# A long convolution by small Fourier transforms: whole fp32 operands in place of high and low parts, and all two-operand work on VectorE

## The chip, the cores and the metric

The kernel runs on one core of a Trainium2 chip. The metric is the device time of one execution in microseconds (us). Five engines work side by side, each through its own queue in order: TensorE (PE in the profile, with its weight loads under PEld), VectorE (DVE), ScalarE (ACT), GpSimd (POOL) and SyncE (SP), which here only issues DMA transfers. Engines wait for each other through semaphores.

## The reference, cut to what matters

The program is a chain of network layers: attention, a recurrent layer, then a second block. In the recurrent layer one branch is a "Hyena" operator: two long convolutions over 1024 positions for each of 512 channels, each followed by a gate.

```python
def fft_long_conv(z, kern, skip):
    L = z.shape[1]
    zf = jnp.fft.rfft(z.astype(jnp.float32), n=2 * L, axis=1)
    kf = jnp.fft.rfft(kern, n=2 * L, axis=0)
    y = jnp.fft.irfft(zf * kf[None], n=2 * L, axis=1)[:, :L]
    return (y + z * skip).astype(z.dtype)

def hyena_operator(u, short_taps, kern, skip):
    v, x1, x2 = split_cols(centred_conv3(u, short_taps), (HY_WIDTH, HY_WIDTH, HY_WIDTH))
    z = v
    for o, gate in enumerate((x1, x2)):
        z = gate * fft_long_conv(z, kern[:, o], skip[o])
    return z
```

Everything is fp32. The kernel spectra `kf` are made much earlier in the program and kept in DRAM.

## The kernel before

The convolution stage is `hyena`. The 512 channels are cut into two halves (`hh`) of 256 and there are two orders (`o`), so four half-convolutions; the second order of a half needs the first order of the same half. Positions are cut into four residues `r` modulo 4, so a transform is eight products with 128 x 128 blocks of a cosine and sine table per residue, and the residues are joined by butterflies.

One half-convolution is a forward part and an inverse part. `hyena_fwd` first brings 256 channels into position-major form: PE transposes into a bank, ACT copies it into `z`, and DVE writes what the copy lost into the low part of `z`. fp32r is a rounded fp32 format; a value of nearly full precision is carried as a high part and a low part, and one product becomes three matmuls (high by high, high by low, low by high). `dft_mm` (L1188) issues these: `F[:, r, part, ...]` is the table, and a product of k = 0, 1 gives six matmuls per output.

Then come two passes (`f` = 0, 1), each with half of the frequencies. A pass loads its kernel spectrum `K` (1 MB), makes four tiles `X[0]` to `X[3]` in four PSUM banks, joins them in `fwd_butterfly` into `Z` (four frequencies groups, real and imaginary part), multiplies `Z` by `K` as complex numbers, applies the inverse butterfly, and writes `G`, again as a high and a low part. The complex product is shared by two engines: POOL makes the two products with the imaginary part of `Z` (L1289, L1291 into `t1`, `t2`), DVE those with the real part (L1290, L1292) and then the two sums (L1294, L1295). ACT copies the result `g` into the high part of `G` (L1311), POOL subtracts to get the low part (L1313; DVE does it in the very last pass).

`hyena_inv` multiplies `G` by the inverse table `I` (again three matmuls per product, L1342), scales and adds (L1346), and gates (L1349 or L1351; for the second order POOL first multiplies the gate by a second one, L1329). The inverse part is a generator that is emitted behind the forward part of the next half, and a scheduler orders each engine's instructions. PSUM: four banks "s" for `X`, two "o" for transposes, two "pt" for the inverse. Most SBUF tiles of a pass (`K`, `Z`, `Y`, `t1`, `t2`, the butterfly's `bx0`, `bx1`, `be`, `by`) have one buffer, `z` too; `G` has three.

The tables `F` and `I` are loaded by POOL's DMA queue at the start of the stage and while the first pass runs (`load_r`, L1028). Behind the stage comes the recurrence (`rwkv_chains`), whose tiles take over the stage's SBUF: POOL clears `LK` (L1702), DVE clears `T`, `eta` and `AE` (L1703 to L1708), SP loads `be`, `LK`, `T`, `SV`.

## Time and profile before

| | us |
|---|---|
| median of 3 runs | 4376.76 (4373.62 to 4385.21) |
| the profiled execution, its own time | 4377.67 |
| its span, first to last instruction | 4375.9 |
| busy over the span: PE, DVE, ACT, POOL | 3884.0, 2828.2, 1794.8, 1452.7 |
| mean granted TensorE clock | 0.928 |

Granted clock is the share of full speed that the TensorE throttle let through. In the profile's rows a group is named by its source line, engine, operation and tiles (output, then inputs, without buffer numbers), then the shape, a count after "x", busy time and mean time of one; in the timeline a row starts with its start time and its length, and ends with the idle time before it and what ended that. "fp32r" is shown as f32 for matmuls.

### The profile page before, as it was taken

How to read it: one execution, taken by the hardware profiler on the slowest of the kernel's cores; microseconds unless marked ns; L12 is line 12 of the kernel's file. 1: busy time of each engine (PE TensorE's matmuls, PEld its weight loads, DVE VectorE, ACT ScalarE, POOL GpSimd, SP SyncE). 2: the span in 40 equal slices, each digit the busy share in tenths (PEclk: the TensorE clock that was granted, in tenths of full speed). 3: DMA queues.
4: the chain of work that ended last, by engine and by line, in shares of the span. 5: the costliest groups of instructions: out<-in, count | busy, mean ns of one | idle time of the engine just before them, and what ended most of it. 6: DMA issues, size and time to landing. Idle time of an engine off the chain costs nothing.

```text
span 4375.9 us, 65931 instructions
## 1 busy us (share of the span) xinstructions
PE 3884.0 (89%) x24045; PEld 3184.5 (73%) x24045; DVE 2828.2 (65%) x5988; ACT 1794.8 (41%) x3754; POOL 1452.7 (33%) x1597
## 2 busy tenths in 40 slices
...
GB/s 206 160 160 157 130 98 163 117 54 31 89 107 145 177 159 140 148 138 60 119 119 104 85 81 127 94 105 121 119 93 191 91 186 65 87 82 77 150 100 78
DMA packets 351340, 515.52 MB, mean 118 GB/s; under 512 B 149863, under 2 KB 226423, under 8 KB 347304
## 3 DMA queue, kind: packets, MB, share of 16 engines
...
## 4 chain that ended last, share of the span: by engine, by line
PE 37%; DVE 7%; DMA 2%; issue 2%; ACT 2%; POOL 1%; SPq 1%; ACTq 0%; DVEq 0%; POOLq 0%
PE bank L285 18%; PE bank L2497 9%; PE bank L2397 2%; DMA SV<-d_V 1%; PE bank L685 1%; PE bank L1745 1%; PE bank L724 1%; PE bank L246 1%; PE bank L1819 1%; PE bank L1757 1%; DVE SV L1813 0%; PE bank L1793 0%; DVE S L694 0%; PE bank L732 0%; PE bank L1775 0%
## 5 line engine op out<-in xcount | busy, mean ns | idle before, releaser
L285 PE MATMUL bank<-hhi,whi 128*128 128x512 f32 (+1 forms) x1264 | 487.6, 386 | 13.0 <-ACT hhi L399 9.9
L285 PE MATMUL bank<-hlo,whi 128*128 128x512 f32 (+1 forms) x1264 | 484.4, 383 | 4.6 <-DVE hlo L400 2.4
L285 PE MATMUL bank<-hhi,wlo 128*128 128x512 f32 (+1 forms) x1264 | 481.5, 381 | 0.0
L267 ACT ACTIVATE whi<-wf 128x1024 fp32r<-128x1024 f32 (+3 forms) x202 | 193.6, 960 | 474.4 <-PE bank L285 395.3
L268 POOL TENSOR_TENSOR wlo<-wf,whi 128x1024 fp32r<-128x1024 f32 (+1 forms) x96 | 221.4, 2308 | 452.8 <-ACT whi L267 418.4
L285 PEld LDWEIGHTS bank<-hhi,whi 128*128 128x128 f32 x1264 | 242.9, 192 | 62.1 <-ACT hhi L399 10.8
L285 PEld LDWEIGHTS bank<-hlo,whi 128*128 128x128 f32 x1264 | 243.0, 192 | 54.8 <-DVE hlo L400 5.1
L285 PEld LDWEIGHTS bank<-hhi,wlo 128*128 128x128 f32 x1264 | 242.7, 192 | 46.4
L2497 PE MATMUL bank<-th,wh 128*128 128x512 f32 x616 | 247.0, 402 | 6.8 <-ACT th L2422 6.8
L2497 PE MATMUL bank<-th,wl 128*128 128x512 f32 x616 | 246.6, 400 | 0.0
L411 POOL CAST phi<-split 128x512 fp32r<-128x512 f32 (+1 forms) x104 | 62.7, 603 | 475.6 <-ACT split L410 380.5
L322 POOL TENSOR_TENSOR walo<-wa,wahi 128x512 fp32r<-128x512 f32 x96 | 137.3, 1444 | 241.6 <-ACT wahi L321 229.8
L285 PE MATMUL bank<-yT,whi 128*128 128x512 f32 (+1 forms) x600 | 191.5, 389 | 0.8 <-ACT rb L386 0.5
L407 DVE TENSOR_TENSOR plo<-bank,phi 128x512 fp32r<-128x512 f32 (+2 forms) x260 | 166.4, 653 | 32.0 <-ACT phi L406 29.6
L406 ACT ACTIVATE phi<-bank 128x512 fp32r<-128x512 f32 (+2 forms) x260 | 143.4, 563 | 65.0 <-PE bank L724 24.0
L1799 POOL TENSOR_SCALAR sp<-SV,PL 64x64 f32<-64x64 f32 x304 | 135.5, 446 | 90.5 <-DVE SV L1813 69.2
L285 PE MATMUL bank<-yH,whi 128*128 128x512 f32 x376 | 151.8, 404 | 9.4 <-ACT ev_a L2160 5.1
L285 PE MATMUL bank<-yB,whi 128*128 128x512 f32 x376 | 151.2, 402 | 7.8 <-DVE yB L397 6.9
L285 PE MATMUL bank<-yH,wlo 128*128 128x512 f32 x376 | 150.9, 401 | 0.0
L268 DVE TENSOR_TENSOR wlo<-wf,whi 128x1024 fp32r<-128x1024 f32 (+2 forms) x106 | 117.6, 1112 | 50.7 <-ACT whi L267 50.5
L2497 PE MATMUL bank<-tl,wh 128*128 128x512 f32 x352 | 141.9, 403 | 5.6 <-DVE tl L2423 4.7
L2497 PEld LDWEIGHTS bank<-th,wh 128*128 128x128 f32 x616 | 117.7, 191 | 36.7 <-ACT th L2422 8.7
...
## 6 DMA issues: line engine op xcount, KB each, us to landing
wf<-in_w_in_dram SPq DMA_DIRECT2D x47, 512.0 KB, 3.7
wf<-in_w_ffn_in_dram SPq DMA_DIRECT2D x44, 512.0 KB, 3.4
d_rec<-r_rec SPq DMA_DIRECT2D x40, 512.0 KB, 3.5
wf<-in_rec_w_in_dram ACTq DMA_DIRECT2D x33, 512.0 KB, 4.1
wf<-in_attn_w_in_dram SPq DMA_DIRECT2D x26, 512.0 KB, 4.4
wa<-in_attn_ada_w_dram POOLq DMA_DIRECT2D x24, 512.0 KB, 4.3
wa<-in_rec_ada_w_dram POOLq DMA_DIRECT2D x24, 512.0 KB, 4.2
...
```

The lines of the kernel that those rows point to most:

```text
L246: self.nc.tensor.matmul(ps_out[:, b * 128:(b + 1) * 128], self.selr[:nb * 4, b, :], rows, start=True, stop=True)
L267: nc.scalar.activation(hi, wf, AF.Copy)
L268: self.wlo.tensor_tensor(lo, wf, hi, OP.subtract)
L285: self.mark = nc.tensor.matmul(ps[:, :n], w[:, k - k0, :], x(k, t0, n), start=(k == ks[0] and j == 0), stop=(k == ks[-1] and j == 2))
L322: nc.gpsimd.tensor_tensor(lo[:, k], w3[:, k], hi[:, k], OP.subtract)
L406: nc.scalar.activation(hi, src, AF.Copy)
L407: nc.vector.tensor_tensor(lo, src, hi, OP.subtract)
L411: nc.gpsimd.tensor_copy(hi, full)
L685: nc.tensor.matmul(bank[:, at:at + n], qs, kk[:, t0:t0 + n], start=(i == 0), stop=(i == 1))
L1799: nc.gpsimd.tensor_scalar(sp[half[h]], sv[half[h], h], pl[half[h]], None, OP.mult)
L2397: nc.tensor.matmul(ps, w[:, k, :], x[:, k, t0:t0 + n], start=(k == k0 and j == 0), stop=(k == k1 - 1 and j == 2))
L2497: self.mark = nc.tensor.matmul(ps, w[i][:, k, :], x[i][k], start=(k == 0 and j == 0), stop=(k == kh - 1 and j == 2))
```

## The change

In the convolution stage, and only there, the transforms take whole fp32 operands. The making of the kernel spectra keeps its high and low parts and the old table, so the program now has the forward table in both forms.

- `F`, `I`, `z` and `G` are fp32 tiles of half the size; each product is one fp32 matmul in place of three fp32r ones. The low part of `z`, ACT's copy into `G` and the subtraction behind it are gone. The table loads are half as large.
- All elementwise work with two operands is on DVE, the gate products included; POOL keeps only its DMA issues in this stage.
- DVE's operations are joined where two have the same shape of work: both rows of a butterfly in one instruction over 1024 elements, the four products of the complex multiplication in two instructions over 2048 (one reads `Z`'s real part twice, the other the imaginary part against `K` with its two parts in reversed order).
- `z`, `K`, `gate` and `sgh` have two buffers; the butterfly's four tiles become `W1` and `W2`.

```diff
-            F = self.t(pf, [128, 4, 2, 1024], F32R, "F")
-            self.reserve(p, ("z", 16, 1), ("K", 8, 1), ("bx0", 2, 1), ("bx1", 2, 1), ("be", 2, 1), ("by", 2, 1), ("Z", 8, 1),
-                         ("Y", 8, 1), ("G", 16, 3))
-            I = self.t(p, [128, 4, 2, 1024], F32R, "I")
+            F = self.t(pf, [128, 4, 1024], F32, "F")
+            self.reserve(p, ("z", 8, 2), ("K", 8, 2), ("W1", 4, 1), ("W2", 4, 1), ("Z", 8, 1), ("T", 8, 1), ("Y", 8, 1), ("G", 8, 3))
+            I = self.t(p, [128, 4, 1024], F32, "I")
...
-        z = self.t(p, [128, 2, 8, 256], F32R, "z")
+        z = self.t(p, [128, 8, 256], F32, "z", bufs=2)
...
-                hi = z[:, 0, q * 4:q * 4 + 4, cc * 128:(cc + 1) * 128]
-                nc.scalar.activation(hi, pv, AF.Copy)
-                nc.vector.tensor_tensor(z[:, 1, q * 4:q * 4 + 4, cc * 128:(cc + 1) * 128], pv, hi, OP.subtract)
+                nc.scalar.activation(z[:, q * 4:q * 4 + 4, cc * 128:(cc + 1) * 128], ps.rearrange("p (j c) -> p j c", c=128), AF.Copy)
...
-            K = self.t(p, [128, 4, 2, 256], F32, "K", bufs=1)
+            K = self.t(p, [128, 4, 2, 256], F32, "K", bufs=2)
...
-                self.dft_mm(X[r][:, 0, :], F, r, f * 128, zr)
-                self.dft_mm(X[r][:, 1, :], F, r, 256 + f * 128, zr)
+                for c in range(2):
+                    for k in range(2):
+                        at = k * 512 + c * 256 + f * 128
+                        self.mark = nc.tensor.matmul(X[r][:, c], F[:, r, at:at + 128], z[:, r * 2 + k], start=(k == 0), stop=(k == 1))
...
-            self.fwd_butterfly(p, X, None, Z)
+            E, O = (self.t(p, [128, 2, 2, 256], F32, n, bufs=1) for n in ("W1", "W2"))
+            nc.scalar.activation(E[:, 1], X[0], AF.Copy)
+            nc.scalar.activation(O[:, 0], X[1], AF.Copy)
+            add(E[:, 0], E[:, 1], X[2])
+            add(E[:, 1], E[:, 1], X[2], OP.subtract)
+            add(O[:, 1, 0], X[3][:, 1], O[:, 0, 1], OP.subtract)
+            add(O[:, 1, 1], O[:, 0, 0], X[3][:, 0], OP.subtract)
+            add(O[:, 0], O[:, 0], X[3])
+            add(Z[:, 0:2], E, O)
+            add(Z[:, 2:4], E, O, OP.subtract)
...
-            nc.gpsimd.tensor_tensor(t1, Z[:, :, 1], K[:, :, 1], OP.mult)
-            nc.vector.tensor_tensor(Y[:, :, 0], Z[:, :, 0], K[:, :, 0], OP.mult)
-            nc.gpsimd.tensor_tensor(t2, Z[:, :, 1], K[:, :, 0], OP.mult)
-            nc.vector.tensor_tensor(Y[:, :, 1], Z[:, :, 0], K[:, :, 1], OP.mult)
+            part = lambda i: Z[:, :, i:i + 1].to_broadcast([128, 4, 2, 256])
+            add(Y, part(0), K, OP.mult)
+            add(T, part(1), K[:, :, ::-1], OP.mult)
...
-            nc.vector.tensor_tensor(g[:, 0], a, b, OP.add)
-            nc.vector.tensor_tensor(g[:, 2], a, b, OP.subtract)
-            nc.vector.tensor_tensor(g[:, 1], c, d, OP.add)
-            nc.vector.tensor_tensor(g[:, 3], c, d, OP.subtract)
...
-            nc.scalar.activation(G[:, 0], g, AF.Copy)
-            (nc.vector if last else nc.gpsimd).tensor_tensor(G[:, 1], g, G[:, 0], OP.subtract)
+            add(G[:, 0:2], ac, bd)
+            add(G[:, 2:4], ac, bd, OP.subtract)
...
-            gate = self.t(p, [128, 1024], F32, "t1" if spare else "gate", bufs=1)
+            gate = self.t(p, [128, 1024], F32, "gate", bufs=2)
...
-                nc.gpsimd.tensor_tensor(gate, gate, sg, OP.mult)
+                nc.vector.tensor_tensor(gate, gate, sg, OP.mult)
...
-                            for gh, fh in ((0, 0), (1, 0), (0, 1)):
-                                nc.tensor.matmul(ps[:, i, :], Gs[f][:, gh, r, half, cc * 128:(cc + 1) * 128],
-                                                 I[:, r, fh, kt * 256:(kt + 1) * 256], start=(n == 0), stop=(n == 11))
+                            nc.tensor.matmul(ps[:, i, :], Gs[f][:, r, half, cc * 128:(cc + 1) * 128],
+                                             I[:, r, kt * 256:(kt + 1) * 256], start=(n == 0), stop=(n == 3))
```

What the scheduler makes of it is seen in the instruction order of each engine. On DVE, a pass from the complex product to the inverse butterfly's end was, before (the second pass of the stage, behind its first product L1290):

```order
L1292 TENSOR_TENSOR Y_18835<-Z_18819,K_18765 128x4x256
L1294 TENSOR_TENSOR Y_18835<-Y_18835,t_4437_18836 128x4x256
L1295 TENSOR_TENSOR Y_18835<-Y_18835,t_4438_18837 128x4x256
L1303 TENSOR_TENSOR Z_18819<-Y_18835 128x256
L1299 TENSOR_TENSOR Z_18819<-Y_18835 128x512
L1300 TENSOR_TENSOR Z_18819<-Y_18835 128x512
L1301 TENSOR_TENSOR Z_18819<-Y_18835 128x512
L1302 TENSOR_TENSOR Z_18819<-Y_18835 128x256
L1305 TENSOR_TENSOR Y_18849<-Z_18819 128x512
L1306 TENSOR_TENSOR Y_18849<-Z_18819 128x512
L1307 TENSOR_TENSOR Y_18849<-Z_18819 128x512
L1308 TENSOR_TENSOR Y_18849<-Z_18819 128x512
```

In the changed kernel the same work (here of the fourth pass; all these operations now go through one helper, so they share line L1271) is:

```order
L1271 TENSOR_TENSOR Y_18916<-Z_18913,K_18882 128x2048
L1271 TENSOR_TENSOR T_18917<-Z_18913,K_18882 128x2048
L1271 TENSOR_TENSOR Y_18916<-Y_18916,T_18917 128x4x256 x2
L1271 TENSOR_TENSOR Z_18913<-Y_18916 128x256
L1271 TENSOR_TENSOR Z_18913<-Y_18916 128x1024
L1271 TENSOR_TENSOR Z_18913<-Y_18916 128x512
L1271 TENSOR_TENSOR Z_18913<-Y_18916 128x256
L1271 TENSOR_TENSOR G_18926<-Z_18913 128x1024 x2
```

Thirteen instructions have become ten, the two products that POOL made are now inside them, and the last two write `G` itself.

On POOL, from the start of the stage, there stood before:

```order
L1234 DMA yH_18614<-d_hy_13427 128x1024 x4
L1028 DMA F_18621<-in_dft_f_dram 128x2048 x4
L1028 DMA I_18631<-in_dft_i_dram 128x2048 x4
L1289 TENSOR_TENSOR t_4422_18744<-Z_18726,K_18669 128x1024
L1291 TENSOR_TENSOR t_4423_18745<-Z_18726,K_18669 128x1024
L1313 TENSOR_TENSOR G_18762<-Y_18757,G_18762 128x2048
L1289 TENSOR_TENSOR t_4437_18836<-Z_18819,K_18765 128x1024
L1291 TENSOR_TENSOR t_4438_18837<-Z_18819,K_18765 128x1024
L1313 TENSOR_TENSOR G_18854<-Y_18849,G_18854 128x2048
```

and now the recurrence's clearing of `LK` follows the table loads at once:

```order
L1235 DMA yH_18614<-d_hy_13427 128x1024 x4
L1030 DMA F_18621<-in_dft_f_dram 128x1024 x4
L1030 DMA I_18630<-in_dft_i_dram 128x1024 x4
L1698 MEMSET LK_4543_19334 128x1536
L1698 MEMSET LK_4545_19338 128x1536
```

Nothing else is left on POOL within the stage. On PE, the forward products of the first half, both passes, were eight tiles of twelve matmuls with `z` moving and `F` stationary, and the transposes of the second half (L1267) came behind them; now the transposes of both halves come first, and then:

```order
L1281 MATMUL bank_4411_18666<-z_18639,F_18621 128x256 x4
L1281 MATMUL bank_4412_18671<-z_18639,F_18621 128x256 x4
L1281 MATMUL bank_4422_18717<-z_18639,F_18621 128x256 x4
L1281 MATMUL bank_4413_18677<-z_18639,F_18621 128x256 x4
L1281 MATMUL bank_4423_18722<-z_18639,F_18621 128x256 x4
L1281 MATMUL bank_4414_18683<-z_18639,F_18621 128x256 x4
L1281 MATMUL bank_4424_18727<-z_18639,F_18621 128x256 x4
L1281 MATMUL bank_4425_18732<-z_18639,F_18621 128x256 x4
```

Four matmuls make a tile in place of twelve. Ahead of the stage the order on every engine is as before. Behind it some neighbouring rows have changed places, in the later part of the recurrence and in the second block's first projections; none was added or removed there.

More of the change, by code (lines that the diff above doesn't have):

```diff
@@ L947, in dft_consts @@
         out.append(np.ascontiguousarray(np.stack([hi, lo], 2).reshape(4, 128, 2, -1)))
-    return out
+        out.append(np.ascontiguousarray(a32.reshape(4, 128, -1)))
+    return out[0], out[1], out[3]
 def hyena_consts():
@@ L1003, in host_b @@
     feats, win = hyena_consts()
-    fwd, inv = dft_consts()
+    fwd, fwd1, inv1 = dft_consts()
     nw = np.ones((128, 2), np.float32)
@@ L1019, in host_b @@
         "hy_b3": np.ascontiguousarray(g("hy_b3")[None]),
-        "feats": feats, "win": win, "dft_f": fwd, "dft_i": inv, "nw": nw, "cmask": cm,
+        "feats": feats, "win": win, "dft_f": fwd, "dft_f1": fwd1, "dft_i1": inv1, "nw": nw, "cmask": cm,
         "rmask": mask_array(),
@@ L1267, in hyena_fwd @@
                     nc.tensor.transpose(ps[:, i * 128:(i + 1) * 128], zr[:, j // 2, (j % 2) * 128:(j % 2) * 128 + 128], self.ident)
-                pv = ps.rearrange("p (j c) -> p j c", c=128)
-                hi = z[:, 0, q * 4:q * 4 + 4, cc * 128:(cc + 1) * 128]
-                nc.scalar.activation(hi, pv, AF.Copy)
-                nc.vector.tensor_tensor(z[:, 1, q * 4:q * 4 + 4, cc * 128:(cc + 1) * 128], pv, hi, OP.subtract)
+                nc.scalar.activation(z[:, q * 4:q * 4 + 4, cc * 128:(cc + 1) * 128], ps.rearrange("p (j c) -> p j c", c=128), AF.Copy)
                 yield
+        add = lambda o, x, y, op=OP.add: nc.vector.tensor_tensor(o, x, y, op)
         for f in range(2):
-            K = self.t(p, [128, 4, 2, 256], F32, "K", bufs=1)
+            K = self.t(p, [128, 4, 2, 256], F32, "K", bufs=2)
             nc.sync.dma_start(K.rearrange("p s c e -> p (s c e)"), self.d_spec[o, hh, f])
@@ L1285, in hyena_fwd @@
+            add(Z[:, 2:4], E, O, OP.subtract)
             yield
             Y = self.t(p, [128, 4, 2, 256], F32, "Y", bufs=1)
[L1287 to L1292 removed]
+            T = self.t(p, [128, 4, 2, 256], F32, "T", bufs=1)
@@ L1293, in hyena_fwd @@
+            part = lambda i: Z[:, :, i:i + 1].to_broadcast([128, 4, 2, 256])
+            add(Y, part(0), K, OP.mult)
+            add(T, part(1), K[:, :, ::-1], OP.mult)
             yield
-            nc.vector.tensor_tensor(Y[:, :, 0], Y[:, :, 0], t1, OP.subtract)
-            nc.vector.tensor_tensor(Y[:, :, 1], Y[:, :, 1], t2, OP.add)
+            add(Y[:, :, 0], Y[:, :, 0], T[:, :, 0], OP.subtract)
+            add(Y[:, :, 1], Y[:, :, 1], T[:, :, 1])
             yield
-            a, b = Z[:, 0], Z[:, 1]
@@ L1298, in hyena_fwd @@
-            c, d = Z[:, 2], Z[:, 3]
-            nc.vector.tensor_tensor(a, Y[:, 0], Y[:, 2], OP.add)
-            nc.vector.tensor_tensor(b, Y[:, 1], Y[:, 3], OP.add)
-            nc.vector.tensor_tensor(c, Y[:, 0], Y[:, 2], OP.subtract)
-            nc.vector.tensor_tensor(d[:, 0], Y[:, 1, 1], Y[:, 3, 1], OP.subtract)
-            nc.vector.tensor_tensor(d[:, 1], Y[:, 3, 0], Y[:, 1, 0], OP.subtract)
-            g = self.t(p, [128, 4, 2, 256], F32, "Y", bufs=1)
-            nc.vector.tensor_tensor(g[:, 0], a, b, OP.add)
@@ L1306, in hyena_fwd @@
-            nc.vector.tensor_tensor(g[:, 2], a, b, OP.subtract)
-            nc.vector.tensor_tensor(g[:, 1], c, d, OP.add)
-            nc.vector.tensor_tensor(g[:, 3], c, d, OP.subtract)
-            yield
-            G = self.t(p, [128, 2, 4, 2, 256], F32R, "G", bufs=3)
-            nc.scalar.activation(G[:, 0], g, AF.Copy)
-            last = o == 1 and hh == 1 and f == 1
-            (nc.vector if last else nc.gpsimd).tensor_tensor(G[:, 1], g, G[:, 0], OP.subtract)
+            ac, bd = (x.rearrange("p (u v) c e -> p u v c e", u=2)[:, :, i] for x, i in ((Z, 0), (Z, 1)))
@@ L1314, in hyena_fwd @@
+            add(Z[:, 0:2], Y[:, 0:2], Y[:, 2:4])
+            add(Z[:, 2], Y[:, 0], Y[:, 2], OP.subtract)
+            add(Z[:, 3, 0], Y[:, 1, 1], Y[:, 3, 1], OP.subtract)
+            add(Z[:, 3, 1], Y[:, 3, 0], Y[:, 1, 0], OP.subtract)
+            G = self.t(p, [128, 4, 2, 256], F32, "G", bufs=3)
+            add(G[:, 0:2], ac, bd)
+            add(G[:, 2:4], ac, bd, OP.subtract)
             Gs.append(G)
@@ L1321, in hyena_inv @@
             ct = hh * 2 + cc
-            spare = o == 1 and hh == 1 and cc == 1
-            gate = self.t(p, [128, 1024], F32, "t1" if spare else "gate", bufs=1)
+            gate = self.t(p, [128, 1024], F32, "gate", bufs=2)
             row = (1 + o) * 512 + ct * 128
```

11 lines of the change are left out of this document (4 added, 7 removed).

## The prediction

> **What bounds the kernel now.** The change lies in one stage, so I read that stage and not the page's shares. The busy time of the engines over the stage (stretch, its length, busy time and instructions of PE, PEld, DVE, ACT, POOL, then granted clock, DMA share, GB/s):
>
> ```profile
> 1850.00:2110.00 260.00, 140.25 (x848) 131.84 (x848) 208.53 (x227) 43.26 (x51) 112.58 (x58) 0.70 0.29 104
> ```
>
> DVE is busy for 208.5 of 260 us; no other engine comes near. But much of that is not work. The groups by line, in the stage alone (busy time, mean ns, idle time before):
>
> ```profile
> L1290 DVE TENSOR_TENSOR Y<-Z,K 128x1024 f32<-128x1024 f32 x8 | 26.4, 3296 | 12.3 <-POOL G L1313 12.3
> L1292 DVE TENSOR_TENSOR Y<-Z,K 128x1024 f32<-128x1024 f32 x8 | 22.7, 2834 | 0.0
> L1346 DVE SCALAR_TENSOR_TENSOR yH<-bank,rn,yH 128x512 f32<-128x512 f32 x16 | 18.3, 1146 | 7.9 <-PE bank L1342 7.9
> L1221 DVE TENSOR_TENSOR Z<-bx,by 128x512 f32<-128x512 f32 x8 | 14.2, 1774 | 0.0
> ...
> L1271 DVE TENSOR_TENSOR z<-bank,z 128x512 fp32r<-128x512 f32 x16 | 10.6, 684 | 7.2 <-ACT z L1270 7.2
> ...
> L1295 DVE TENSOR_TENSOR Y<-Y,t 128x1024 f32<-128x1024 f32 x8 | 9.7, 1212 | 0.0
> ...
> L1207 DVE TENSOR_TENSOR be<-bx,bank 128x512 f32<-128x512 f32 x8 | 5.5, 685 | 18.4 <-PE bank L1193 18.2
> ...
> L1210 DVE TENSOR_TENSOR by<-bank,bx 128x256 f32<-128x256 f32 x8 | 3.4, 420 | 1.7 <-PE bank L1193 1.4
> ...
> L1313 DVE TENSOR_TENSOR G<-Y,G 128x2048 fp32r<-128x2048 f32 x1 | 2.7, 2739 | 2.1 <-ACT G L1311 2.1
> ```
>
> The same kind of operation over 1024 elements takes 1212 ns at L1295 and 3296 ns at L1290, which runs beside POOL's two-input products; over 512 elements it takes 685 ns at L1207 and 1774 ns on average at L1221, which often stands beside POOL's subtraction into `G`. Two engines slow each other there. The waits show the second half of the trouble, the way from `g` to PE (who waited for whom, us, times, longest):
>
> ```profile
> POOL G L1313 <- ACT G L1311: 81.6, 6, 17.2
> ACT G L1311 <- DVE Y L1308: 76.0, 6, 24.3
> ...
> PE bank L1342 <- ACT G L1311: 43.9, 6, 18.4
> ...
> DVE Y L1290 <- POOL G L1313: 12.3, 4, 4.4
> ```
>
> `G` goes DVE, ACT, POOL, PE, and the next product on DVE stands behind POOL. So the stage is a loop over eight passes whose length DVE sets, with POOL in it. Its length, from the first and the last of the eight L1290, and the stage's last DVE work with the recurrence's first behind it:
>
> ```profile
> 1884.85 2.85 DVE L1290 TENSOR_TENSOR Y<-Z,K 128x1024 f32<-128x1024 f32 x1
> ...
> 2067.54 3.36 DVE L1290 TENSOR_TENSOR Y<-Z,K 128x1024 f32<-128x1024 f32 x1
> ...
> 2102.38 1.23 DVE L1351 SCALAR_TENSOR_TENSOR yH<-yH,t 128x1024 f32<-128x1024 f32 x1
> 2103.71 1.50 DVE L1703 MEMSET T<- 128x768 f32 x2
> ```
>
> Seven intervals in 182.7 us are **26.1 us a pass**, and 36.1 us are left from the last L1290 to the end of the stage at 2103.6.
>
> **The change, part by part: DVE.** DVE starts its next instruction a little before the last one's record ends, so I price by start to start:
>
> ```profile
> 1916.14 1.21 DVE L1294 TENSOR_TENSOR Y<-Y,t 128x1024 f32<-128x1024 f32 x1
> 1917.28 1.21 DVE L1295 TENSOR_TENSOR Y<-Y,t 128x1024 f32<-128x1024 f32 x1
> 1918.41 0.41 DVE L1303 TENSOR_TENSOR Z<-Y 128x256 f32<-128x256 f32 x1
> 1918.75 0.68 DVE L1299 TENSOR_TENSOR Z<-Y 128x512 f32<-128x512 f32 x1
> 1919.35 0.68 DVE L1300 TENSOR_TENSOR Z<-Y 128x512 f32<-128x512 f32 x1
> ```
>
> 1.13 us for 1024 elements, 0.60 for 512, 0.33 for 256. No undisturbed row has 2048 elements. From below, 1.13 plus twice the step of 0.53 is 2.19; from above, the one DVE row of 2048 elements (L1313) has 2.74, part of it beside POOL. I take 2.25, near the line through three undisturbed sizes; the upper end costs 16 x 0.5 = 8 us. The broadcast and the reversed order leave runs of 256 neighbours, so I add nothing for them.
>
> A pass then costs DVE 4 x 0.60 + 4 x 0.33 + 7 x 1.13 + 2 x 2.25 = 16.1 us. The inverse adds 3.25 us for each of eight column blocks (two L1346 at 1.06, one gate at 1.13), 3.25 a pass; the four gate products moved from POOL add 4.5 in all, 0.6 a pass. Together **20.0 us a pass** with a little for steps that wait for the one before. At the same prices, without POOL beside it, the old pass is 14 x 0.60 + 4 x 0.33 + 4 x 1.13 = 14.2, with `z`'s low parts (1.2) and the inverse 18.7. So the change gives DVE slightly more work; what it takes away is the collision with POOL and the wait for POOL. From the first product to the last: 7 x (26.1 - 20.0) = **-43 us**, if nothing else needs more than 20 us a pass.
>
> **PE.** A whole fp32 product stands in the trace elsewhere, and leaves two records. The nearest rows: 128 columns on 128 x 128 weights at L1610, 512 columns at L1082 in the cold start with fp32r matmuls of 512 columns (L328) behind it; and this stage's fp32r matmuls of 256 columns:
>
> ```profile
> 1390.46 1.05 PE L1610 MATMUL bank<-r_rec,r_bdx 128*128 128x128 f32 x8
> 1391.27 0.48 PE L285 MATMUL bank<-hlo,whi 128*128 128x512 f32 x1
> ...
> 8.22 3.67 PE L1082 MATMUL bank<-ft,w 33*64 33x512 f32 x4 [8.22 <-DMA ft<-in_feats_dram]
> ...
> 12.21 0.63 PE L328 MATMUL bank<-walo,sc 128*4 128x512 f32 x1
> 12.63 0.63 PE L328 MATMUL bank<-wahi,sc 128*4 128x512 f32 x1
> ...
> 1866.91 2.90 PE L1193 MATMUL bank<-z,F 128*128 128x256 f32 x12 [3.83 <-DMA F<-in_dft_f_dram]
> ...
> 1977.23 3.04 PE L1193 MATMUL bank<-z,F 128*128 128x256 f32 x24 [0.53 <-DVE bx L1208]
> ...
> 1982.75 4.33 PE L1342 MATMUL bank<-I,G 128*128 128x256 f32 x34 [2.24 <-POOL G L1313]
> ```
>
> L1610's four products take 0.81 us until the next matmul starts, or (1.05 - 0.28)/7 = 0.11 us a record: 0.20 to 0.22 for 128 columns, so 0.41 to 0.44 us for 256 if it goes by columns. L1082 says it does: 3.67/2 = 1.83 us for 512 columns, four times L328's 0.42 us from start to start, and 0.92 us for 256 columns at that slow clock. From below, a cost set by weights alone would be 0.22. Three fp32r matmuls cost 3 x 3.04/24 = 0.38 us in the fast row and 3 x 2.90/12 = 0.73 in the slow one. So PE's array work goes **up**, by about 0.06 us for each of 256 products at full clock and 0.19 at the slow one.
>
> Which clock? The granted clock of three stretches (PEclk is the number behind POOL's):
>
> ```profile
> 1870.00:1876.00 6.00, 5.51 (x26) 5.51 (x27) 0.00 (x0) 0.44 (x1) 0.00 (x0) 0.51 0.59 231
> 1876.00:1882.00 6.00, 5.76 (x49) 5.56 (x49) 3.04 (x6) 0.60 (x1) 2.11 (x4) 1.00 0.79 243
> ...
> 1977.00:1988.00 11.00, 7.61 (x60) 7.23 (x60) 10.87 (x12) 2.03 (x3) 8.20 (x3) 1.00 0.01 1
> ```
>
> After 3.83 us of idleness the clock is half for some 9 us; after waits of 0.53 and 2.24 us it stays full. Each pass has 32 products. At 0.44 they take 14 us, at 0.50 (a little slow time mixed in) 16, and eight transposes about 1.2 (eight slow ones: 1.95):
>
> ```profile
> 1855.06 1.95 PE L1267 MATMUL bank<-ident,yH 128*128 128x128 f32 x8 [5.18 <-DMA yH<-d_hy]
> ```
>
> That is 17 of DVE's 20 us. The idle time that is left comes in pieces of 2 to 4 us, where the 80 us ahead of L1342 came in pieces of up to 18. I take 0.50: PE hides under DVE. It becomes the bound above (20.0 - 1.2)/32 = **0.58 us a product**, which is the clock at half for about a third of the time.
>
> The Trainium skill, "TensorE: Matmul & The Clock Gate", Part 1 (the HAM clock gate), says that an idle window of about 3.4 us puts the clock at half and about as long of work restores it. By that rule gaps of 4 us would each cost slow products, which is the rival on the clock below; the slow 9 us after 3.83 us of idleness agree with the first half of it, and are longer than the second.
>
> **What is around the loop.** At the start PE waits for `F` (the row at 1866.91). The table is half as large, but the second buffers let SP ask at once for another `K`, `gate` and `sgh`:
>
> ```profile
> K<-d_spec SPq DMA_DIRECT2D x8, 1024.0 KB, 4.8
> F<-in_dft_f_dram POOLq DMA_DIRECT2D x4, 1024.0 KB, 17.8
> ...
> gate<-d_hy SPq DMA_DIRECT2D x7, 512.0 KB, 4.0
> ```
>
> 2 MB less and 1 + 0.5 + 0.5 MB more: I expect `F` within 2 us of before, and 24 products, slow at first, until the first butterfly is complete at about 1881 (L1211 and its neighbours there now): **0**. At the end, from the last product: 4.5 for the two products, one gate, 2.3 sums, 2.7 butterfly, 2.3 into `G`, 13 us; then PE, idle for 14 us before and so slow at first, has 28 products, 10 at 0.88 and 18 at 0.44, 17 us; then 2.3 for scaling and gate. 32 against 36.1: **-4**.
>
> ACT loses `G`'s copy (it stands in the path today) and has 43 us of work in 260. POOL has no operand work left; its clearing of `LK` moves forward beside DVE: 0 if such a clear leaves DVE alone, as it does here, where L1346 takes its usual time beside four of them; 3 us at most.
>
> ```profile
> 2100.45 5.33 POOL L1702 MEMSET LK<- 128x1536 f32 x4 [8.93 <-PE bank L1342]
> ...
> 2101.14 1.13 DVE L1346 SCALAR_TENSOR_TENSOR yH<-bank,rn,yH 128x512 f32<-128x512 f32 x1 [1.71 <-PE bank L1342]
> ```
>
> The recurrence's start follows DVE's last instruction as before (the clears of `T`, `eta`), so the gain passes on. The swapped rows later on I put at 0, between -4 and +4.
>
> **Sum.** -43 + 0 - 4 = -47 us. The profiled execution took 4377.67 us (span 4375.9 and 1.8 around it), 0.9 above the median of 4376.76: 4331 against it, **4330** against the median.
>
> **Rivals.** (1) *The clock stays as it is.* With the stage's mean of 0.70, a product costs 0.44/0.70 = 0.63 us, 21.3 us a pass: PE sets the pass, 7 x 4.8 = -34, tail -2: 4341. For: fp32 keeps gaps at 4 us, on the edge of the slow clock. Against: the fast rows after 2.24 us. (2) *PE becomes the bound at the slow clock, and the kernel gets slower.* Place: all 256 products; it decides from 0.58 us on. From `F` at 1866.9: 256 x 0.88 + 64 transposes at 1.95/8 = 241, and 4 to 6 where PE must wait for the first and last `G` and the end: 2112 to 2114 against 2103.6: +10, 4387. For: each product needs more array time. Against: a PE so busy has no idle time that would slow it. (3) *The change doesn't free DVE*: the long broadcast products run as slowly as the disturbed ones (3.3 us for 1024, so 6.6 each), 28.7 a pass, 7 x 2.6 = +18 and +5 in the tail: 4400. Against: nothing runs beside them. (4) *The gain is lost on the way*: loads or clears of the recurrence come late, or the swapped rows cost; half of the gain, 4355 to 4370.
>
> **Chances.** Forecast (DVE at about 20 us a pass, 4316 to 4339) 0.62; (1), up to 4352, 0.23; (2) 0.05; (3) 0.03; (4) 0.07. The low end has PE at 0.44 throughout, `F` 4 us earlier and PE warm in the tail (-58); the high end lets PE set some passes and takes DVE's 2048 elements at 2.74. Range 4314 to 4354. 0.3% (about 13 us) is what a measurement of this kernel can tell from no change; below 4364 lie the forecast, (1) and most of (4): faster 0.90, same 0.07, slower 0.03.
>
> **What would show it.** Right: no POOL work but clears in the stage; DVE's operations at 0.68 and 1.21 us without long ones, the 2048 ones at 2.3; eight pairs of products about 20 us apart; PE records of about 0.21 us start to start with granted clock above 0.85; DVE's idle time in the loop near zero. Wrong: DVE waiting for PE banks in every pass (rival 1 or 2), products well over 2.7 us (3), or the recurrence's first clear early but its end not (4). An fp32 product at 256 columns that isn't twice L1610's would unsettle the PE part.

## The result, and the profile after

| | before | after |
|---|---|---|
| median, us | 4377.41 (4373.62 to 4385.21, 4 runs) | 4325.86 (4318.2 to 4327.2, 4 runs) |
| the profiled execution, its own time | 4377.67 | 4318.2 |
| its span | 4375.9 | 4316.1 |

The ratio is 0.9876, with a 95% interval of 0.9858 to 0.9894: 46 to 62 us less. The prediction was 4330 in a range of 4314 to 4354. The profiled execution of after is the fastest of its four, so I compare stages first and come back to the rest below.

The busy time of the engines over the changed kernel's loop (first to last product into `Y`), its tail, and the whole stage (columns as in the prediction):

```profile
1888.27:2025.04 136.77, 105.15 (x424) 86.49 (x424) 136.36 (x141) 16.53 (x26) 2.71 (x2) 0.85 0.22 77
2025.04:2054.27 29.23, 15.19 (x56) 12.56 (x56) 19.69 (x17) 0.00 (x0) 8.50 (x10) 0.70 0.09 30
1854.68:2054.27 199.59, 143.84 (x576) 118.45 (x576) 161.91 (x165) 27.24 (x41) 17.59 (x24) 0.81 0.30 110
```

The first row says it all: DVE is busy for 136.36 of 136.77 us. The same stretch of before, from the first to the last L1290:

```profile
1884.85:2067.54 182.69, 103.70 (x628) 97.76 (x628) 167.82 (x184) 31.37 (x35) 81.77 (x24) 0.73 0.19 70
```

The groups of the changed stage, by line and shape. All of DVE's two-operand work has L1271, the line of the helper `add`, so one reads by tiles:

```profile
L1271 DVE TENSOR_TENSOR G<-Z 128x1024 f32<-128x1024 f32 x16 | 18.9, 1231 | 0.1
L1271 DVE TENSOR_TENSOR Z<-W,W 128x1024 f32<-128x1024 f32 x16 | 18.9, 1227 | 0.2
L1271 DVE TENSOR_TENSOR Y<-Y,T 128x1024 f32<-128x1024 f32 x16 | 18.9, 1225 | 0.0
L1271 DVE TENSOR_TENSOR Y<-Z,K 128x2048 f32<-128x2048 f32 x8 | 18.4, 2297 | 0.2
...
L1342 DVE SCALAR_TENSOR_TENSOR yH<-bank,rn,yH 128x512 f32<-128x512 f32 x16 | 18.3, 1148 | 9.4 <-PE bank L1338 9.4
L1271 DVE TENSOR_TENSOR W<-W,bank 128x512 f32<-128x512 f32 x24 | 16.0, 688 | 24.9 <-PE bank L1281 24.9
```

No shape has a long mean any more: 1.23 us for 1024 elements where L1290 had 3.30, 2.30 for 2048. What idle time DVE has left lies ahead of the loop (24.9, waiting for the first `X`) and in the tail (9.4).

The stage's parts in the profiled executions, from timeline rows. The stage starts at the end of the last L285 on PE and ends with the last gate. The lead-in lasts from its start to the first product into `Y` on DVE, the loop from there to the last one, the tail from the last one to the stage's end. "Pass" is a seventh of the loop, "recurrence" the time from the stage's end to the last L1815 (L1819 before) on PE. Runs of the experiments stand with them; each ratio is to before in the same set of runs. In e2 and e5 products into `t1` on DVE go ahead of that into `Y` (1.1 us at the first, 3.4 at e2's last), so their parts shift by that much and the stage does not:

| kernel | lead-in | loop | pass | tail | stage | recurrence | median us | ratio (95%) |
|---|---|---|---|---|---|---|---|---|
| before | 34.97 | 182.69 | 26.10 | 36.07 | 253.7 | 407.6 | 4377.41 | 1 |
| after | 33.59 | 136.77 | 19.54 | 29.23 | 199.6 | 399.4 | 4325.86 | 0.9876 (0.9858 to 0.9894) |
| e1 after again | 33.65 | 136.76 | 19.54 | 29.26 | 199.7 | 404.6 | 4323.58 | 0.9874 (0.9860 to 0.9889) |
| e2 all on DVE, nothing else | 35.68 | 162.41 | 23.20 | 28.32 | 226.4 | 403.2 | 4357.87 | 0.9946 (0.9928 to 0.9963) |
| e3 fp32 operands, nothing else | 31.73 | 146.37 | 20.91 | 31.54 | 209.6 | 408.8 | 4340.70 | 0.9911 (0.9893 to 0.9928) |
| e4 after, T on POOL | 33.72 | 144.71 | 20.67 | 31.52 | 210.0 | 413.3 | 4347.04 | 0.9934 (0.9914 to 0.9954) |
| e5 e2 and e3 together | 32.91 | 138.40 | 19.77 | 27.64 | 198.9 | 414.8 | 4335.41 | 0.9893 (0.9871 to 0.9915) |
| e6 after, fp32r high parts only | 31.27 | 138.86 | 19.84 | 19.37 | 189.5 | 397.3 | 4311.06 | 0.9839 (0.9817 to 0.9862) |
| e7 after, forward products twice | 41.15 | 149.98 | 21.43 | 27.63 | 218.8 | 407.5 | 4345.30 | 0.9916 (0.9891 to 0.9941) |
| e8 before again | 34.58 | 182.46 | 26.07 | 35.78 | 252.8 | 407.7 | 4382.59 (one run) | |
| e9 after, sum on PE and ACT | 34.16 | 133.07 | 19.01 | 32.50 | 199.7 | 406.1 | 4328.22 | 0.9877 (0.9854 to 0.9900) |
| e10 after, F first | 24.11 | 136.91 | 19.56 | 28.12 | 189.1 | 402.8 | 4314.96 | 0.9852 (0.9834 to 0.9870) |
| e11 after, 18 unread products | 33.56 | 136.73 | 19.53 | 29.27 | 199.6 | 407.9 | 4328.22 | 0.9883 (0.9865 to 0.9900) |
| e12 F first, 24 unread products | 25.04 | 136.89 | 19.56 | 26.41 | 188.3 | 408.0 | 4317.79 | 0.9864 (0.9844 to 0.9884) |

The stage's parts repeat within 1 us (before and e8, after and e1). The time of a whole execution scatters by 6 to 22 us within one set of runs.

### The profile page after: what moved, and what is told of

It is laid out like the page before. It is cut to its first block, busy times and chain, and to the rows that moved or that the text cites. A ratio compares the mean times of both kernels' runs of the same rounds, so it can differ in the third digit from the quotient of the medians.

```text
span 4316.1 us, 65300 instructions
## 1 busy us (share of the span) xinstructions
PE 3887.0 (90%) x23789; PEld 3168.0 (73%) x23789; DVE 2779.1 (64%) x5935; ACT 1781.4 (41%) x3746; POOL 1357.6 (31%) x1570
## 4 chain that ended last, share of the span: by engine, by line
PE 37%; DVE 7%; DMA 2%; ACT 2%; issue 1%; POOL 1%; SPq 1%; ACTq 0%; DVEq 0%; POOLq 0%
PE bank L285 18%; PE bank L2493 10%; PE bank L2393 2%; DMA SV<-d_V 1%; PE bank L1741 1%; PE bank L1789 1%; PE bank L724 1%; PE bank L1815 1%; PE bank L1753 1%; PE bank L685 1%; PE bank L246 0%; DVE d L2225 0%; DVE S L694 0%; DVE SV L1809 0%; DVE junk L2225 0%
## 5 line engine op out<-in xcount | busy, mean ns | idle before, releaser
L285 PE MATMUL bank<-hhi,whi 128*128 128x512 f32 (+1 forms) x1264 | 488.6, 387 | 13.1 <-ACT hhi L399 10.1
L285 PE MATMUL bank<-hlo,whi 128*128 128x512 f32 (+1 forms) x1264 | 485.0, 384 | 4.3 <-DVE hlo L400 2.1
L285 PE MATMUL bank<-hhi,wlo 128*128 128x512 f32 (+1 forms) x1264 | 482.6, 382 | 0.0
L285 PEld LDWEIGHTS bank<-hhi,whi 128*128 128x128 f32 x1264 | 243.8, 193 | 62.7 <-ACT hhi L399 10.9
L285 PEld LDWEIGHTS bank<-hlo,whi 128*128 128x128 f32 x1264 | 243.7, 193 | 54.5 <-DVE hlo L400 4.6
L285 PEld LDWEIGHTS bank<-hhi,wlo 128*128 128x128 f32 x1264 | 242.9, 192 | 46.7
L285 PE MATMUL bank<-yT,whi 128*128 128x512 f32 (+1 forms) x600 | 190.6, 387 | 1.1 <-ACT ush L1393 0.5
L285 PE MATMUL bank<-yH,whi 128*128 128x512 f32 x376 | 151.4, 403 | 7.9 <-ACT ev_a L2156 4.4
L285 PE MATMUL bank<-yB,whi 128*128 128x512 f32 x376 | 150.6, 401 | 8.0 <-DVE yB L397 7.2
L285 PE MATMUL bank<-yH,wlo 128*128 128x512 f32 x376 | 150.4, 400 | 0.0
```

The costliest lines, as they stand in the source:

```text
L285: self.mark = nc.tensor.matmul(ps[:, :n], w[:, k - k0, :], x(k, t0, n), start=(k == ks[0] and j == 0), stop=(k == ks[-1] and j == 2))
```

## The experiments

**Is what lies outside the stage part of the change? (e1, e8)** Both kernels once more, without an edit.

> The changed kernel once more, unchanged. In the two profiled executions the stage is 54.1 us shorter, but the stretch ahead of it 4.8 us longer and the recurrence behind it 8.3 us shorter (407.3 to 399.0). If these two are a property of the kernel (rows that moved in the recurrence), they come again within 2 us. If they are scatter between executions, the stretch ahead of the stage comes back to about 1850 and the recurrence to 403 to 408, and the whole is near the median of 4326; the stage itself stays at 198 to 202 us in both cases.

> The kernel before once more, for the scatter of the parts outside the stage: two executions of the changed kernel gave 1854.7 and 1856.5 ahead of the stage and 399.4 and 404.6 for the recurrence, the one execution of before 1849.9 and 407.6. If the parts outside are the same in both kernels, before gives 1850 to 1857 and 398 to 408 this time, and the stage itself 252 to 256; if the change costs 5 us ahead of the stage, 1850 again within 1 us.

The stage came out at 199.7 and 252.8. What lies around it is scatter: the stage began at 1856.5 in e1 and at 1858.0 in e8, against 1849.9 in the first execution of before. The recurrence of the changed kernel took 399.4 and 404.6, and 407.9 in e11, whose instructions there stand in the same order on every engine; before has 407.6 and 407.7. So at most some 4 us could be the rows that moved, and it is no more than the scatter of one order.

**Which part brings it? (e2, e3, e5)** In e2 only POOL's work moves, with high and low parts and single buffers as before:

```diff
-            nc.gpsimd.tensor_tensor(t1, Z[:, :, 1], K[:, :, 1], OP.mult)
+            nc.vector.tensor_tensor(t1, Z[:, :, 1], K[:, :, 1], OP.mult)
...
-            nc.gpsimd.tensor_tensor(t2, Z[:, :, 1], K[:, :, 0], OP.mult)
+            nc.vector.tensor_tensor(t2, Z[:, :, 1], K[:, :, 0], OP.mult)
...
-            (nc.vector if last else nc.gpsimd).tensor_tensor(G[:, 1], g, G[:, 0], OP.subtract)
+            nc.vector.tensor_tensor(G[:, 1], g, G[:, 0], OP.subtract)
...
-                nc.gpsimd.tensor_tensor(gate, gate, sg, OP.mult)
+                nc.vector.tensor_tensor(gate, gate, sg, OP.mult)
```

> The kernel before with one thing done alone: the two products t1 and t2, G's low part and the gate product go from POOL to DVE; high and low parts, single buffers and unjoined operations stay. My theory (the collision and the wait for POOL are the loss): DVE has 18.7 + 2 x 1.13 + 2.25 + 0.6 = 23.8 us a pass, all undisturbed, against 26.1: 7 x 2.3 = -16 us, 4361 (4352 to 4368). Rival (DVE's amount of work is the loss, POOL's help is worth what it takes over): 5.1 us more in each pass, +36 us, 4412.

The groups of e2:

```profile
L1313 DVE TENSOR_TENSOR G<-Y,G 128x2048 fp32r<-128x2048 f32 x8 | 18.3, 2292 | 0.6 <-ACT G L1311 0.6
...
L1290 DVE TENSOR_TENSOR Y<-Z,K 128x1024 f32<-128x1024 f32 x8 | 9.8, 1224 | 0.0
```

DVE has some 5 us more to do in each pass and the loop is 20 us shorter (16 were expected): L1290 takes 1224 ns in place of 3296, and the wait for POOL ahead of it is gone. The rival (more work on DVE, +36 us) is out.

In e3 the operands are whole, and POOL keeps `t1`, `t2` and the gate product:

```diff
-            g = self.t(p, [128, 4, 2, 256], F32, "Y", bufs=1)
+            g = self.t(p, [128, 4, 2, 256], F32, "G", bufs=3)
...
-            G = self.t(p, [128, 2, 4, 2, 256], F32R, "G", bufs=3)
-            nc.scalar.activation(G[:, 0], g, AF.Copy)
-            last = o == 1 and hh == 1 and f == 1
-            (nc.vector if last else nc.gpsimd).tensor_tensor(G[:, 1], g, G[:, 0], OP.subtract)
-            Gs.append(G)
+            Gs.append(g)
```

> The kernel before with whole fp32 operands alone: one product for three, no low part of z, g goes to PE as DVE wrote it (no copy on ACT, no subtraction on POOL); t1, t2 and the gate product stay on POOL, nothing is joined, single buffers. My theory: DVE 18.7 - 1.2 = 17.5 us a pass, and 3.7 us more because two products still run beside POOL's (3.30 and 2.83 for 1.21 each): 21.2 to 22 us a pass, 7 x 4.1 to 4.9 = -29 to -34 and -4 in the tail: 4338 to 4344. Rival (the work that is all on one engine and joined is what brings it): 24 us or more a pass, 4360. Rival (the collision costs nothing by itself): 17.5 us a pass, 4312.

4340.70 and 20.91 us a pass, a little under the 21.2 to 22 expected: the largest single part, 44 of the stage's 54 us, although the products with `K` still collide (the second one on DVE took 3101 ns in the mean). It can't be added to e2's 27 us: both edits take POOL's subtraction into `G`, and the wait for it, out of the loop. e5 does both:

> As the kernel with whole fp32 operands alone, and t1, t2 and the gate product on DVE too: what is left against the changed kernel are the joined operations and the second buffers. By prices DVE has 17.5 + 2 x 1.13 + 0.6 = 20.4 us a pass (19.9 if prices are as much too high as in the changed kernel), no record over 1.3 us for 1024 elements. My theory: pass 19.9 to 20.5, the time 4325 to 4333. Rival (joining and second buffers carry a good part of the gain): pass above 21.5, time above 4338.

Pass 19.77, stage 198.9, against 19.54 and 199.6 of the changed kernel. Joining the operations and the second buffers are worth 1.6 us in the loop and nothing in the stage: its two lengths differ by less than the 1 us within which they repeat. The time, 4335, missed the 4325 to 4333. In the profiled execution, the longest of its four (4343.93), the stage began 7 us later than in e1 and the recurrence took 10 us more (414.8); its instructions stand in another order here. Whether that order costs anything or this is scatter is left open: the interval of e5 overlaps that of the changed kernel.

**What is the collision? (e4)** The changed kernel with one long product on POOL:

```diff
-            add(T, part(1), K[:, :, ::-1], OP.mult)
+            nc.gpsimd.tensor_tensor(T, part(1), K[:, :, ::-1], OP.mult)
```

> The changed kernel with one product of 2048 elements (T) on POOL beside DVE's (Y). My theory (two engines with two-input work slow each other): Y takes 4.5 to 6.5 us in place of 2.3 and the sums behind wait for T, so a pass is 0.5 to 2 us longer than 19.5 though DVE has 2.25 us less to do: +4 to +14 us. Rival (amount of work): a pass is 17.3 us, -15 us.

A pass is 1.1 us longer with 2.25 us less work on DVE; the stage 10.3 longer. The time is 23 us up on e1, of which the 10 us in the stage are explained; the recurrence (413.3, again another order) has 9 us of the rest (against e1) and wasn't taken apart. Rows of the timeline of e4, POOL's `T` first, then DVE's `Y` of the same pass, for two passes:

```profile
1946.82 6.57 POOL L1299 TENSOR_TENSOR T<-Z,K 128x2048 f32<-128x2048 f32 x1 [19.40 <-DVE Z L1271]
...
1965.45 4.53 POOL L1299 TENSOR_TENSOR T<-Z,K 128x2048 f32<-128x2048 f32 x1 [12.06 <-DVE Z L1271]
```

```profile
1946.72 2.29 DVE L1271 TENSOR_TENSOR Y<-Z,K 128x2048 f32<-128x2048 f32 x1
1953.42 2.36 DVE L1271 TENSOR_TENSOR Y<-Y,T 128x1024 f32<-128x1024 f32 x2 [4.41 <-POOL T L1299]
...
1966.30 5.83 DVE L1271 TENSOR_TENSOR Y<-Z,K 128x2048 f32<-128x2048 f32 x1
```

The two do not slow each other by some factor, as the prediction had it: one shuts the other out. In the first of these passes DVE began 0.1 us earlier and took its usual 2.29 us; POOL took 6.57, its 4.53 and DVE's 2.04 ahead of them. In the second POOL began first and took 4.53; DVE's product ended at 1972.13, which is 2.15 after POOL's end. All eight pairs are of one of these kinds. The kernel before shows the same on its own products, POOL's two first, then DVE's two:

```profile
1909.43 2.39 POOL L1289 TENSOR_TENSOR t<-Z,K 128x1024 f32<-128x1024 f32 x1
1911.78 3.36 POOL L1291 TENSOR_TENSOR t<-Z,K 128x1024 f32<-128x1024 f32 x1
```

```profile
1909.51 3.39 DVE L1290 TENSOR_TENSOR Y<-Z,K 128x1024 f32<-128x1024 f32 x1 [1.79 <-POOL G L1313]
1912.83 3.40 DVE L1292 TENSOR_TENSOR Y<-Z,K 128x1024 f32<-128x1024 f32 x1
```

The four take turns: L1289 ends at 1911.82, L1290 at 1912.90, L1291 at 1915.14 and L1292 at 1916.23. DVE ends 1.1 us behind POOL each time, which is the length of its product alone.

The Trainium skill, "SBUF — State Buffer", section "Who interferes with whom", states this: a DVE instruction with two SBUF inputs and a GpSimd one that reads SBUF exclude each other for a whole instruction, and issue order decides who waits. The rows agree, and so does the other half, that a GpSimd instruction that only writes is no bar. In the changed kernel POOL clears `LK` from 2029.59 to 2032.28, and the two sums on DVE beside it take their usual 2.35 us:

```profile
2029.59 2.69 POOL L1698 MEMSET LK<- 128x1536 f32 x2 [20.65 <-DVE T L1271]
```

```profile
2030.58 2.35 DVE L1271 TENSOR_TENSOR Y<-Y,T 128x1024 f32<-128x1024 f32 x2
```

**Does PE lie under DVE? (e6, e7)** In e6 the tables, `z` and `G` are fp32r, one product each (the edit of `F` is shown; the low parts are left out of the sums). In e7 each forward product is issued twice.

```diff
-            F = self.t(pf, [128, 4, 1024], F32, "F")
+            F = self.t(pf, [128, 4, 1024], F32R, "F")
```

```diff
-                for c in range(2):
+                for c in (0, 1) * 2:
                     for k in range(2):
```

> The changed kernel with one fp32r product in place of one fp32 product (tables rounded to their high parts, z and G written as fp32r; the low parts are left out of the computation). PE's cost of a product falls from 0.44 to about 0.13 us at full clock. My theory (PE lies under DVE in the loop): the passes stay at 19.3 to 19.7 us; only where PE is waited for does the stage get shorter: lead-in -5 to -9 (24 products at half clock), tail -6 to -9 (28 products): -11 to -18 us in all. Rival (PE shares in setting the pass): passes under 18.5 us, -20 us or more.

> The changed kernel with each forward product issued twice into the same bank (the second set starts the sum anew): 16 products more in a pass. My theory puts the point where PE sets the pass at about (19.5 - 1.2)/32 = 0.57 us a product; 48 products at 0.44 are 21.1, with transposes 22.3 us a pass, at the 0.50 of the prediction 25.2: pass 21.5 to 25, +14 to +38 in the loop and +6 to +12 in the lead-in. Rival (PE is far from the bound, its fp32 products cost less than counted): pass under 20.5.

The loops of e6 and of e7, as windows:

```profile
1888.75:2027.60 138.85, 51.30 (x228) 44.18 (x228) 137.99 (x141) 16.57 (x26) 2.77 (x2) 0.60 0.23 80
```

```profile
1897.67:2047.65 149.98, 139.52 (x646) 121.55 (x644) 138.92 (x142) 16.66 (x26) 2.71 (x2) 0.97 0.21 74
```

PE's busy time in the loop halves in e6 and the loop does not get shorter (2.1 us longer: one gate product more, 1.2 us, falls into it), at a clock of 0.60: with so little work on PE the clock doesn't matter there. In e7 PE is busy for 139.5 of 150 us, and DVE waits 5.5 us for PE's banks and 4.9 for a gate's load: 21.43 us a pass, just under the 21.5 expected. Of e7's 646 records in the loop 32 are transposes and 614 belong to 307 products; in the changed kernel it is 32 and 392, so 196 products. So PE begins to set the pass at about half again as many products. In e6 the tail fell by 9.9 us, more than expected, but the lead-in only by 2.4, so the stage by 10.2 where 11 to 18 were expected: with PE out of the way the lead-in waits for transfers. PE's rows of e6 in the lead-in:

```profile
1875.06 1.20 PE L1281 MATMUL bank<-z,F 128*128 128x256 f32 x4 [0.58 <-DMA F<-in_dft_f_dram]
...
1883.52 2.08 PE L1281 MATMUL bank<-z,F 128*128 128x256 f32 x8 [1.73 <-DMA F<-in_dft_f_dram]
```

**The lead-in's transfers (e10).** The DMA engines are full from 1860 to 1878 in e1 (three of the windows, 3 us each):

```profile
1860.00:1863.00 3.00, 1.28 (x6) 1.31 (x7) 0.00 (x0) 0.14 (x1) 1.36 (x3) 0.50 1.02 408
...
1872.00:1875.00 3.00, 2.44 (x9) 1.91 (x8) 0.00 (x0) 2.09 (x3) 0.00 (x0) 0.50 1.02 418
1875.00:1878.00 3.00, 3.00 (x11) 2.47 (x10) 0.00 (x0) 0.61 (x2) 0.00 (x0) 0.66 1.04 425
```

PE's first forward products there:

```profile
1874.02 15.73 PE L1281 MATMUL bank<-z,F 128*128 128x256 f32 x64 [0.56 <-DMA F<-in_dft_f_dram]
```

Much of this is needed only later: the second `K`, `gate` and `sgh`, which the second buffers let SP ask for, but also the first `gate` and `sgh` and half of `yH`, which the kernel before asked for as early. e10 makes all of these wait (`pace` adds a dependency of the later instruction on the earlier one; `mark` is the last forward product; `sgh` is paced like `gate`):

```diff
-            for r in range(4):
+            for r in range(2):
                 nc.gpsimd.dma_start(yH[:, r], d_hy[r * 128:(r + 1) * 128, :])
+            for r in range(4):
                 self.load_r(F[:, r], A["dft_f1"][r])
...
+            if f == 1:
+                self.pace(dk, self.mark)
...
+                if self.late is not None:
+                    for k in (2, 3):
+                        self.pace(nc.gpsimd.dma_start(yH[:, k], self.late[k * 128:(k + 1) * 128, :]), self.mark)
+                    self.late = None
...
-            nc.sync.dma_start(gate, d_hy[row:row + 128, :])
+            self.pace(nc.sync.dma_start(gate, d_hy[row:row + 128, :]), self.mark)
```

> The changed kernel with the lead-in's transfers put in another order: of yH only the two column blocks that the first transform needs go ahead of F; the other two, the second K, gate and sgh wait for the first forward products. Theory (in the lead-in the transfers end last: the DMA engines are full, 420 GB/s, from 1860 to 1878, with 8 MB to move, and the products wait for F at 1874): the first product starts 5 to 8 us earlier, the first butterfly too: lead-in 33.6 to 25.5 to 29; the loop 0 to 3 us longer where K or gate come late. Rival (the half clock of PE sets the lead-in, F was there in time): lead-in 32 or more.

PE in e10:

```profile
1868.69 1.95 PE L1270 MATMUL bank<-ident,yH 128*128 128x128 f32 x8 [2.14 <-DMA yH<-d_hy]
1870.48 11.27 PE L1285 MATMUL bank<-z,F 128*128 128x256 f32 x48
```

The first forward product starts 11.0 us after the stage's start (1859.5), against 17.5 in e1 (1874.0 and 1856.5), and waits for nothing. The second buffers are the smaller part of that: without them, in e3 and e5, it starts 15.8 and 15.9 us after the stage's start. The lead-in fell by 9.5 us, a little more than expected, and the loop did not pay for it. With 4314.96 this is the fastest kernel of the study that computes everything; the stage is 10.5 us shorter, the whole 8.6 by the medians (e1), with intervals that overlap.

**The clock in the tail (e11, e12).** Products that nobody reads fill PE's idle time ahead of the last `G`; e12 has `range(12)` and the edit of e10 too:

```diff
+        if o == 1 and hh == 1:
+            for k in range(9):
+                ps = self.bank("s", (128, 2, 256))
+                for i in range(2):
+                    nc.tensor.matmul(ps[:, i], Gs[0][:, k % 4, i, :128], I[:, k % 4, :256], start=True, stop=True)
```

> The changed kernel with 18 products more on PE, whose results nobody reads, between the last but one and the last G, so that PE works through most of its 12.3 us of idle time ahead of the last 28 products. Theory (these 28 run at half clock at first, 15.2 us): at full clock 28 x 0.44 = 12.3 us, tail 29.2 to about 26.4 (25.9 to 27.2), nothing else changes in the stage. Rival (idle time does not set the clock): tail 29 again, or longer by the products that are in the way.

> The two together: transfers of the lead-in in the order of the run before last, and now 24 products nobody reads (in place of 18, which left 3.94 us of idle time ahead of the last 28 and the same 15.2 us for them). By the rows, 24 leave 3.94 - 6 x 0.445 = 1.3 us. Theory (idle time of about 4 us already puts the clock at half, 1.3 us does not, as after 1.1 us in the lead-in): 28 products in 12.3 to 12.8 us, tail 28.1 to 25.2 to 25.8; lead-in 24 to 25, loop 137, stage 186 to 187, the time 4308 to 4318. Rival (the slow start of the last 28 has another cause, the first use of the last G, say): tail 28 again.

The last 28 products (two records each) in the changed kernel, in e11 and in e12:

```profile
2036.66 15.19 PE L1338 MATMUL bank<-I,G 128*128 128x256 f32 x56 [12.30 <-DVE G L1271]
```

```profile
2035.89 15.22 PE L1343 MATMUL bank<-I,G 128*128 128x256 f32 x56 [3.94 <-DVE G L1271]
```

```profile
2028.12 12.35 PE L1351 MATMUL bank<-I,G 128*128 128x256 f32 x56 [1.85 <-DVE G L1273]
```

e11 missed: an idle time of 3.94 us costs as much as one of 12.30, so its tail is the rival's 29 again. The rival's reason falls with e12: with 1.85 us left, e12 has the full clock from the first product, 12.35 us as expected, and the tail is 1.7 us shorter than that of e10 (28.12); I had expected 2.3 to 2.9. In e10 the same products took 14.08 us after the same 12.30 of idleness, so there was less to gain:

```profile
2032.13 14.08 PE L1346 MATMUL bank<-I,G 128*128 128x256 f32 x56 [12.30 <-DVE G L1273]
```

The whole time doesn't show the gain: the stage is 0.8 us shorter than in e10, and the recurrence was 5 longer.

**Can DVE be relieved further? (e9)** `D` holds diagonals made at the stage's start; the gate then reads `ev`, which ACT writes.

```diff
+                    nc.tensor.matmul(ps[:, i, :], self.D[:, o * 4 + ct], zsr[:, r, :], start=True, stop=False)
...
-                nc.vector.scalar_tensor_tensor(zsr[:, rp * 2:rp * 2 + 2, :], ps, self.rn[:, o, ct:ct + 1],
-                                               zsr[:, rp * 2:rp * 2 + 2, :], OP.mult, OP.add)
+                nc.scalar.activation(evr[:, rp * 2:rp * 2 + 2, :], ps, AF.Copy, scale=self.rn[:, o, ct:ct + 1])
```

> The changed kernel with the inverse's scaled sum taken off DVE: the old values, times skip over rn, are added in PSUM by one more fp32 product with a diagonal of 128x128 for each output (32 products in all), ACT reads the bank with the scale rn into a tile of its own, and DVE has only the gate left. Theory (DVE alone sets the loop, it had no idle time in it): 12 operations of 1.06 us from start to start fall away between the first and the last product: loop 136.8 to about 124 (121 to 128), 17.7 us a pass, and -1 to -3 in the tail; stage 182 to 188. Rival (PE with 24 more products in the loop, 10.6 us at 0.44, takes over): loop above 132.

The loop was 133.1, beyond 132, and the stage not shorter at all. Rows of the tail, where ACT waits for PE and DVE for ACT:

```profile
2054.68 1.17 ACT L1350 ACTIVATE ev<-bank,rn 128x512 f32<-128x512 f32 x1 [4.10 <-PE bank L1346]
```

```profile
2055.89 1.23 DVE L1354 SCALAR_TENSOR_TENSOR yH<-ev,gate 128x1024 f32<-128x1024 f32 x1 [9.30 <-ACT ev L1350]
```

ACT's eviction, its copy out of PSUM, took 1.17 us, not the 0.6 that I had taken from its other copies of 512 elements. DVE's idle time in the loop is 6.9 us (5.0 for `ev`, 1.9 for `X`), and more of the next pass's work falls into the loop, one gate product among it. In the tail 34 products take the place of 28. PE wasn't busy throughout, so the rival's name for it is only half right: the way from the last `G` through PE and ACT to the gate is now what is waited for. PE's own rows there show one reason, a product with `D` (two records) and four of the others:

```profile
2046.60 1.06 PE L1341 MATMUL bank<-yH,D 128*128 128x256 f32 x2
2047.48 1.91 PE L1346 MATMUL bank<-I,G 128*128 128x256 f32 x8
2049.22 1.06 PE L1341 MATMUL bank<-yH,D 128*128 128x256 f32 x2
```

The product with `D` takes 0.88 us until the next one starts, twice the 0.44 that was counted; the four others take 1.74. It is of the same shape, but its moving operand is every fourth element of a row of `yH`. So the 24 in the loop cost PE some 21 us and not 10.6. The stride as the cause was not tried alone.

## Why the prediction was right

- **What bounds the kernel.** Right: the collision and the wait for POOL, not the amount of work. e2 shows it by itself. The picture of it was loose: 3.3 us at L1290 was no slower operation but 1.1 us of work behind a POOL instruction (e4, and the rows of before beside it).
- **DVE's price of a pass.** 1.13, 0.60 and 0.33 us held, and 2048 elements cost 2.20 from start to start (2025.04 to 2027.24 below) against the 2.25 taken. The step that was mis-sized is the inverse: 3.25 us a pass over seven passes is 22.8, but only six of the eight column blocks lie between the first and the last product, as the group of the loop alone shows (two L1342 to a block):

```profile
L1342 DVE SCALAR_TENSOR_TENSOR yH<-bank,rn,yH 128x512 f32<-128x512 f32 x12 | 13.7, 1149 | 0.0
```

  With six blocks (19.5), three gate products (3.4) and 7 x 16.1 = 112.7 the sum is 135.6, and the loop took 136.8: -45.9 in place of -43. The 1.2 us between the two are not accounted for.
- **PE.** 0.44 us a product at full clock held: 24 records took 5.34 us, 0.22 each. At a clock of 0.50, from 2037.2 on, the records of the last 28 products start 0.43 us apart.

```profile
1956.71 5.34 PE L1338 MATMUL bank<-I,G 128*128 128x256 f32 x24
```

  It lies under DVE with 105 of 137 us busy. Here too a step was counted too large: the loop holds 196 products, 28 a pass and not 32. Without 6.1 us of transposes they come to some 99 us, 0.51 each, against the 0.50 taken. The idle time was not all in pieces of 2 to 4 us: pieces of 4.34, 4.61 and 7.59 us stand in the loop, and slow products behind them. The granted clock that I named as a sign, above 0.85, was 0.85 in the loop and 0.81 in the stage; DVE's idle time of 0.4 us in the loop shows that it did not matter. Rivals (1) and (2) needed PE to set the pass; e6 and e7 put that point at about half again as many products.
- **Lead-in.** 0 expected, -1.4 found. The reason given held, 2 MB less of tables and 2 MB more asked for early: the first product starts 17.5 us after the stage's start, against 17.0 in the kernel before. The 1.4 us come behind it, where the way to the first product into `Y` takes 16.1 us in place of 17.9. e10 shows that the early transfers were not needed so early.
- **Tail.** -4 expected, -6.8 found. Two parts were too dear. The last 28 products were put at 17 us with ten of them at the slow clock; they took 15.19. And they start 11.6 us after the last product into `Y` (2036.66), not 13: PE begins before the second of the two operations into `G` ends, at 2037.74. Rows of DVE from the last product on:

```profile
2025.04 2.29 DVE L1271 TENSOR_TENSOR Y<-Z,K 128x2048 f32<-128x2048 f32 x1
2027.24 2.29 DVE L1271 TENSOR_TENSOR T<-Z,K 128x2048 f32<-128x2048 f32 x1
...
2035.38 2.36 DVE L1271 TENSOR_TENSOR G<-Z 128x1024 f32<-128x1024 f32 x2
...
2053.05 1.22 DVE L1347 SCALAR_TENSOR_TENSOR yH<-yH,gate 128x1024 f32<-128x1024 f32 x1
```

- **Rival (3)**, long products as slow as disturbed ones, is out with 2297 ns. **Rival (4)**, a gain lost behind the stage: nothing was lost in the changed kernel. In e4 and e5 the recurrence stood 5 to 15 us above the three executions of the changed order (399.4 to 407.9), but in e6, e9, e10 and e12, in other orders again, it took 397.3 to 408.0. Such a loss is possible, and not settled.
- **Sum.** -47 expected; -54 in the stage (253.7 to 199.6) and 46 to 62 by the whole. The three parts miss in the same direction (2.9, 1.4 and 2.8 us), so nothing cancels in the stage. That the whole comes nearer, 52 us by the medians, is scatter outside the stage and luck. What joining and the second buffers add was counted neither as gain nor as loss; in the stage the runs show none (e5).
